# A two-layer diffusion backbone on one core: inputs fetched at once, a selector made on the chip, idle matmuls during the loads, and a new order of issue

## The chip, the core and the metric

The kernel runs on one NeuronCore of a Trainium2 chip. The metric is the device time of one launch in microseconds (us). A profile is one execution recorded by the hardware profiler; its span runs from the core's first instruction to its last, and the launch's own time is a little longer than the span. The engines are called as the profile calls them: PE is TensorE's matmuls, PEld its weight loads, DVE is VectorE, ACT is ScalarE, POOL is GpSimd, and SP is the queue that issues every DMA here.

## What is computed

A latent of 512 tokens by 1024 features and a context of 256 tokens pass two layers. Layer 0 mixes tokens by windowed grouped attention (16 query heads, 4 key heads of 64, band of 384 keys plus all 256 context keys, a sink logit for each head); layer 1 mixes them by a chunked gMLP. A SwiGLU network with 2816 hidden features follows each. RMS norms stand before and after each part, and a modulation (shift, scale, gate) comes from a conditioning vector through a 1024 by 6144 matrix for each layer. Only the latent is returned, and the context's own result of layer 0 is not needed.

```python
for i in range(DEPTH):
    mod_l = silu(c) @ ada_w[i] + ada_b[i]          # sh, sc, g for the mixer and for the FFN
    mod_c = silu(c_ctx) @ ada_w[i] + ada_b[i]
    h_l = modulate(rmsnorm(x, norm_g[i, 0]), sh_ml, sc_ml)
    h_c = modulate(rmsnorm(ctx, norm_g[i, 0]), sh_mc, sc_mc)     # layer 0
    y_l = mixer(h_l, h_c)                           # attention in layer 0, gMLP in layer 1
    x = x + g_ml * rmsnorm(y_l, norm_g[i, 1])
    f_l = swiglu(modulate(rmsnorm(x, norm_g[i, 2]), sh_fl, sc_fl), ffn_w_in[i], ffn_w_out[i])
    x = x + g_fl * rmsnorm(f_l, norm_g[i, 3])
return x
```

## The kernel before

All tensors are float32. A large product is made of three matmuls on a reduced-precision type: each operand is split into a high part (a cast, on ACT) and a low part (the difference, on DVE or POOL), and `mm3` (L216 to L219) or `mm_a` (L221 to L225) adds high by high, high by low and low by high in PSUM. So each 128 by 1024 half of a weight unit needs a DMA into a `raw` buffer (two of them, shared with the modulation's matrices), `Stream.high` on ACT (L173) and `Stream.low` on DVE or POOL (L176).

**The first stage** ends with the keys, values and first queries. The six 128-token tiles (four of x, two of the context) come by `x_fetch` (L409) into buffers of the tag `stg`, of which there are four. Each is squared on ACT (`square_in`, L191), gets its reciprocal root on DVE and POOL (`rstd_in`, L198 and L201), is multiplied by it on DVE (`norm_in`, L422), turned by eight 128 by 128 transposes on PE (`turn_in`, L431) and copied out of PSUM (`turned_in`, L438 and L443). For each of eight groups k of 128 features, `ada0_fetch` brings a 1 MB piece of the modulation matrix, `ada0_rows` (L454) multiplies it by the conditioning vectors, four groups of PE columns at a time, `ada0_rows_out` (L459) copies the partial rows, `ada0_cols` (L465) adds them and turns them into columns by a product with the selector `sel`, and `ada0_done` (L471, L472) makes scale and shift. `modulate0` (L480) applies them to group k of the latent on DVE, `modulated_high` casts the result on ACT, `modulated_low` takes the rest on DVE; the `_ctx` steps (L492) do the same for the context with tiles `hfc` and `hc`. Then `kv` (L217 to L219) adds group k's share to the keys and values of six tiles, and `q_first` that of the first queries. `sel` is a 128 by 2 tile, zero but for four rows in each quarter, which come by four DMAs of 4 by 2 numbers.

**The attention stage** makes 16 blocks of scores (L813, L814), bounds (L820), exponentials (L825), normalised probabilities (`normalise`, L841 on POOL), transposes (L847, L854) and values (L867), with the queries of the next heads (`q_step`, into `q_ps`) between them. The weight units of the queries are 2 to 5; their low parts are made on POOL in quarters of 128 by 512. **The first down projection** (`down`, L1090) follows: `work` steps add the attention's output into `y`, a `Chain` for each of four token tiles adds it to x (L1052), normalises and shifts (L1064, L1068), turns the tile (L1075) and splits it into H (`turned_hi` on ACT, `turned_lo` on DVE), and `head` starts the SwiGLU on tile after tile (`fa`). In the chains of tiles 2 and 3 a `merge` (L1036) comes first.

**The order** of the first stage, the attention and the first down projection is written out by hand. Every step is put into `plan` with `at(time, step)` (L519), and `run_plan` (L527) issues the steps in the order of the table `ORDER` (L41 to L156). What the table says is the order on each engine's queue and on SP's; engines then run freely and wait for each other by semaphores. The rest of the program (the two SwiGLU networks and the gMLP) is in plain code order.

## Time and profile before

| | us |
|---|---|
| median of three runs | 1191.85 |
| lowest and highest run | 1189.71, 1191.92 |
| the profiled execution's own time | 1185.71 |
| its span | 1183.9 |
| PE busy | 1150.2 |
| DVE, ACT and POOL busy | 648.9, 448.6, 205.0 |

A row of the profile's timeline, or of its chain of waits, begins with the start in us from the span's start and the duration in us; then come engine, line, operation, and the tiles written and read. In a row of the chain `issue` is time in which the engine waited for nothing that the profile shows. A row of the windows view gives, for a stretch of time, the busy time of each engine with its count of instructions, the granted TensorE clock as a share of full speed, the mean busy share of the 16 DMA engines, and GB/s. Matmuls are pipelined: a 128 by 512 matmul lasts 0.39 us in the timeline, but at full clock the next starts 0.23 us after it.

### The profile page before, as it was taken

To read this page: it belongs to the slowest core of one execution; us is meant where nothing else is said; L and a number is where in the kernel's file an instruction comes from. 1 tells how busy PE (TensorE), PEld (TensorE's weight loads), DVE (VectorE), ACT (ScalarE), POOL (GpSimd) and SP (SyncE) were. 2 spreads that over 40 slices of the span, in tenths; PEclk is the share of its full clock that TensorE was granted. 3 is DMA by queue.
4 is the path that set the end of the run, shared out by engine and by line. 5 is a ranking of instruction groups with operands and counts; after the bars stand their busy time and mean duration, and the time that the engine had idled before them with its cause. 6 is when DMAs were issued, how large, how long until landed. Compare 5 with 4: busy or idle time off the path is not lost.

```text
span 1183.9 us, 14683 instructions
## 1 busy us (share of the span) xinstructions
PE 1150.2 (97%) x5904; PEld 955.5 (81%) x5904; DVE 648.9 (55%) x902; ACT 448.6 (38%) x726; POOL 205.0 (17%) x187
## 2 busy tenths in 40 slices
PE   5999999999999999999999899999999999999997
PEld 4789888678988888888888788888888888878886
DVE  4788988866454657633446656546463223323234
ACT  6347677654322322322323444245122222213222
POOL 1437456417000000000003413024000000000000
PEclk9999999999999999999999899999999999999999
DMA  8742331252254576634343243231362232232221
GB/s 325 266 164 90 113 107 67 72 182 86 77 212 175 183 279 227 235 108 142 109 145 138 90 165 112 80 107 36 110 224 98 102 107 102 77 106 76 103 71 71
DMA packets 24744, 157.98 MB, mean 133 GB/s; under 512 B 3290, under 2 KB 3546, under 8 KB 7396
## 3 DMA queue, kind: packets, MB, share of 16 engines
q1 hardware_dynamic: 24676, 157.04, 37.7%
q8 instruction: 46, 0.75, 0.2%
q14 instruction: 22, 0.18, 0.0%
HBM read 154.94 MB, written 2.10 MB: 133 GB/s over the span
## 4 chain that ended last, share of the span: by engine, by line
PE 66%; issue 18%; DVE 8%; DMA 3%; ACT 2%; POOL 2%; DVEq 0%; POOLq 0%; SPq 0%; ACTq 0%
PE y L225 12%; PE f L1249 10%; PE f L1248 10%; PE f L1250 10%; PE v L225 3%; PE o_ps L867 2%; PE pT_ps L847 2%; PE s_ps L813 2%; PE fa L219 1%; PE s_ps L814 1%; DVE x L1052 1%; DMA ada_raw<-in_ada 1%; PE fa L217 1%; PE fa L218 1%; PE q_ps L217 1%
## 5 line engine op out<-in xcount | busy, mean ns | idle before, releaser
L176 DVE TENSOR_TENSOR w_lo<-w_raw,w_hi 128x1024 fp32r<-128x1024 f32 x149 | 183.3, 1237 | 321.2 <-ACT w_hi L173 318.7
L173 ACT CAST w_hi<-w_raw 128x1024 fp32r<-128x1024 f32 x162 | 168.8, 1052 | 460.3 <-PE f L1249 258.6
L225 PE MATMUL y<-w_hi,st 128*128 128x512 f32 x928 | 250.6, 390 | 2.8 <-DVE act L1235 2.8
L1248 PE MATMUL f<-H,w_hi 128*128 128x512 f32 x640 | 249.5, 390 | 0.0
L1250 PE MATMUL f<-H,w_lo 128*128 128x512 f32 x640 | 249.2, 389 | 0.0
L1249 PE MATMUL f<-H,w_hi 128*128 128x512 f32 x640 | 249.0, 389 | 0.0
L225 PEld LDWEIGHTS y<-w_hi,st 128*128 128x128 f32 x928 | 173.8, 188 | 39.1 <-DVE act L1235 3.2
L225 PE MATMUL y<-w_lo,st 128*128 128x512 f32 x464 | 143.5, 389 | 0.0
L314 DVE SCALAR_TENSOR_TENSOR acc<-ada_raw,sc,acc 128x1024 f32<-128x1024 f32 x80 | 106.0, 1325 | 66.4 <-DMA ada_raw<-in_ada 61.0
L1249 PEld LDWEIGHTS f<-H,w_hi 128*128 128x128 f32 x640 | 120.2, 188 | 25.0
L1250 PEld LDWEIGHTS f<-H,w_lo 128*128 128x128 f32 x640 | 120.1, 188 | 25.0
L1248 PEld LDWEIGHTS f<-H,w_hi 128*128 128x128 f32 x640 | 120.1, 188 | 24.9
L201 POOL TENSOR_TENSOR ry<-ry,mhalf 128x1 f32<-128x1 f32 x16 | 12.3, 771 | 582.9 <-DVE ry L198 579.4
L225 PEld LDWEIGHTS y<-w_lo,st 128*128 128x128 f32 x464 | 87.1, 188 | 18.1
L841 POOL TENSOR_SCALAR p<-p,st 128x512 f32<-128x512 f32 (+1 forms) x64 | 52.8, 840 | 45.8 <-DVE st L837 27.8
L820 DVE CUSTOM_DVE_ANT_0 s_ps<-s_ps,mask,nsink 128x512 f32<-128x512 f32 (+1 forms) x64 | 52.0, 819 | 13.4 <-PE s_ps L814 8.6
L825 ACT ACTIVATE p<-s_ps,st 128x512 f32<-128x512 f32 (+1 forms) x64 | 47.5, 743 | 16.0 <-DVE st L820 13.4
L305 POOL MEMSET acc<- 128x1024 f32 x10 | 9.5, 953 | 201.3 <-DVE acc_st L176 199.8
L176 POOL TENSOR_TENSOR w_lo<-w_raw,w_hi 128x512 fp32r<-128x512 f32 (+1 forms) x23 | 37.1, 1619 | 31.4 <-ACT w_hi L173 31.4
L847 PE MATMUL pT_ps<-ident,p 128*128 128x128 f32 x288 | 41.4, 273 | 0.2 <-ACT pt L854 0.2
L813 PE MATMUL s_ps<-khi,qT 128*128 128x256 f32 (+1 forms) x128 | 40.5, 329 | 0.2
L219 PE MATMUL fa<-w_lent,H 128*128 128x256 f32 x128 | 36.5, 285 | 4.2 <-DVE H L176 4.1
(201 smaller groups left out, 1685.3 us busy)
## 6 DMA issues: line engine op xcount, KB each, us to landing
w_raw<-in_w SPq DMA_DIRECT2D x87, 1024.0 KB, 4.8
ada_raw<-in_ada SPq DMA_DIRECT2D x40, 1024.0 KB, 4.9
ada<-in_ada SPq DMA_DIRECT2D x8, 1024.0 KB, 7.4
row<-in_norm_g SPq DMA_DIRECT2D x7, 512.0 KB, 6.1
xin<-in_x SPq DMA_DIRECT2D x4, 512.0 KB
x<-in_x SPq DMA_DIRECT2D x4, 512.0 KB, 3.6
out<-x SPq DMA_DIRECT2D x3, 512.0 KB, 2.6
xin<-in_ctx SPq DMA_DIRECT2D x2, 512.0 KB, 4.8
```

The lines of the kernel that those rows point to most:

```text
L173: nc.scalar.copy(out=hi, in_=src)
L176: (eng or nc.vector).tensor_tensor(out=lo, in0=src, in1=hi.bitcast(F32), op=ALU.subtract)
L219: nc.tensor.matmul(dst, ll, rh, start=False, stop=last)
L225: nc.tensor.matmul(dst, l, w[:, n * 512:(n + 1) * 512], start=first and i == 0, stop=last and i == 2)
L314: nc.vector.scalar_tensor_tensor(out=ac, in0=w, scalar=sc[:, k:k + 1], in1=ac, op0=ALU.mult, op1=ALU.add)
L813: nc.tensor.matmul(dst, self.qT[:, j, :], khi[:, self.g, k0:k0 + (c1 - c0) * P], start=True, stop=False)
L820: nc.vector.tensor_tensor_reduce(out=s, in0=s, in1=self.msk, scale=-1.0, scalar=nsink[:, h:h + 1], op0=ALU.add, op1=ALU.min, accum_out=sel ...
L841: nc.gpsimd.tensor_scalar(out=p, in0=p, scalar1=self.st[:, 12 + j:13 + j], scalar2=1.0, op0=ALU.mult, op1=ALU.mult)
L847: nc.tensor.transpose(ps[:, j * P:(j + 1) * P], self.probs[j][:, i * P:(i + 1) * P], ident)
L1248: nc.tensor.matmul(dst, hi, H[:, k, :], start=k == 0, stop=False)
L1249: nc.tensor.matmul(dst, hi, H[:, KC + k, :], start=False, stop=False)
L1250: nc.tensor.matmul(dst, lo, H[:, k, :], start=False, stop=k == KC - 1)
```

## The change

The tiles of the context go into buffers of their own (tag `vec`), so that all six input tiles are fetched without waiting for a buffer. `sel` comes out of the identity matrix, by two additions on DVE in place of a memset and four DMAs. A zeroed tile `idle` feeds matmuls into PSUM tiles that are written over later: five `warm` steps of 128 by 512, and one of 128 by 256 before the first transposes of a context tile and before the first `ada0_rows`. `norm_in` works on half tiles. `turned_in` makes one copy of 128 by 512 in place of two of 128 by 256, and which engine makes it changes. `modulated_high` makes H's high part on ACT from the transposed x with scale and shift, no longer from DVE's `hf`, which stays for the low part. The keys' rotation writes in place and one addition writes both copies; the context's keys are copied twice on ACT instead of once on ACT and once on DVE; the keys are split in halves. The table `ORDER` is another for all that it covers.

The core of the diff (of the table, its first line):

```diff
-x_fetch_1 x_fetch_2 square_in_2 square_in_1 x_fetch_3 dma#2 square_in_3 dma ada0_fetch_0 rstd_in_2 <lambda>
...
     sel = base.tile([P, 2], F32, name="sel")
-    nc.vector.memset(sel, 0.0)
...
-    xnT = [vec(f"xnT{i}") for i in range(4)]
+    xnT = [big(f"xnT{i}") for i in range(2)]
...
     def x_fetch(t):
-        xin[t] = base.tile([P, D], F32, name="xin", tag="stg", bufs=4)
+        xin[t] = base.tile([P, D], F32, name="xin", tag="stg", bufs=4) if t < NT else vec("xin")
...
-    def norm_in(t):
-        nc.vector.tensor_scalar(out=xin[t], in0=xin[t], scalar1=r0[t], scalar2=None, op0=ALU.mult)
+    def norm_in(t, h):
+        v = xin[t][:, h * 512:(h + 1) * 512]
+        nc.vector.tensor_scalar(out=v, in0=v, scalar1=r0[t], scalar2=None, op0=ALU.mult)
...
+    idle = first_p.tile([P, SEQ], F32, name="idle")
+    nc.vector.memset(idle, 0.0)
+
+    def fill(ps):
+        nc.tensor.matmul(ps, idle[:, 0:P], idle[:, 0:ps.shape[-1]], start=True, stop=True)
+
+    def warm(i):
+
+        if i == 0:
+            turned["warm"] = bankA("warm")
+        fill(turned["warm"])
...
+        if t == 4 and h == 0:
+            fill(ps[:, 0:256])
...
+        copy = nc.scalar.copy if t == 1 or t > 2 and h == 0 else nc.vector.tensor_copy
         if t < NT:
-            for q in range(2):
-                (nc.vector.tensor_copy if t % 2 else nc.scalar.copy)(
-                    out=xnT[2 * h + q].rearrange("p (k s) -> p k s", k=2)[:, :, t * P:(t + 1) * P],
-                    in_=pv[:, 2 * q:2 * q + 2, :])
+            copy(out=xnT[h].rearrange("p (k s) -> p k s", k=4)[:, :, t * P:(t + 1) * P], in_=pv)
         else:
-            c = slice((t - NT) * P, (t - NT + 1) * P)
-            nc.scalar.copy(out=cnT[:, 4 * h:4 * h + 4, c], in_=pv)
+            copy(out=cnT[:, 4 * h:4 * h + 4, (t - NT) * P:(t - NT + 1) * P], in_=pv)
+
+    def select():
+
+        i4 = ident.rearrange("p (q s) -> p q s", q=4)[:, :, 0:4:2]
+        s2 = small(4, "sel2").rearrange("p (q z) -> p q z", q=2)
+        nc.vector.tensor_tensor(out=s2, in0=i4[:, 0:2, :], in1=i4[:, 2:4, :], op=ALU.add)
+        nc.vector.tensor_tensor(out=sel, in0=s2[:, 0, :], in1=s2[:, 1, :], op=ALU.add)
...
     def modulated_high(k):
-        high(HA[:, k, :], h_mod[k])
+        xk = xnT[k // 4][:, (k % 4) * 512:(k % 4 + 1) * 512]
+        nc.scalar.activation(out=HA[:, k, :], in_=xk, func=AF.Identity, scale=sb0[k][:, 2:3], bias=sb0[k][:, 0:1])
...
-    for q in range(4):
-        at(0, dma, sel[32 * q:32 * q + 4, :], a["sel"])
+    for i in range(5):
+        at(.01 * i, warm, i)
+    at(4, select)
...
-            src = kv_part(t, 0).rearrange("p t (h d) -> p t h d", h=KVH)
-            nc.scalar.copy(out=doubled(t, 0), in_=src)
-            nc.vector.tensor_copy(out=doubled(t, 1), in_=src)
+            for z in range(2):
+                nc.scalar.copy(out=k_rows[t][:, z * 512:(z + 1) * 512].rearrange("p (h w d) -> p h w d", h=KVH, w=2),
+                               in_=kv_part(t, 0)[:, z, :].rearrange("p (h d) -> p h d", h=KVH).unsqueeze(2).to_broadcast([P, KVH, 2, HD]))
...
     def k_add(t):
-        m = k_raw[t][:, 512:1024].rearrange("p (t h d) -> p t h d", t=2, h=KVH)
-        for w in (1, 0):
-            nc.vector.tensor_tensor(out=doubled(t, w), in0=doubled(t, 0), in1=m, op=ALU.add)
+        nc.vector.tensor_tensor(out=k_rows[t].rearrange("p (n w d) -> p n w d", w=2, d=HD), in0=twice(k_raw[t][:, 0:512]),
+                                in1=twice(k_raw[t][:, 512:1024]), op=ALU.add)
```

Three places of the new order. **The first loads.** SP's queue from the second row on: `xin` is a tile of x or of the context, `ada_...` a 1 MB piece for one group k, `w_raw` weights of the keys and values. Before:

```order
L170 DMA xin<-in_x 128x1024 x3
L170 DMA cols<-in_cols 128x24
L170 DMA ident<-in_ident 128x128
L170 DMA ada_119<-in_ada 128x2048
L170 DMA xin<-in_x 128x1024
L170 DMA sel<-in_sel 4x2 x4
L170 DMA bu<-in_bu 128x8
L170 DMA xin<-in_ctx 128x1024 x2
L170 DMA ada_169<-in_ada 128x2048
L170 DMA w_raw<-in_w 128x1024
```

And now:

```order
L171 DMA xin<-in_ctx 128x1024
L171 DMA xin<-in_x 128x1024
L171 DMA ident<-in_ident 128x128
L171 DMA xin<-in_ctx 128x1024
L171 DMA cols<-in_cols 128x24
L171 DMA xin<-in_x 128x1024 x3
L171 DMA ada_183<-in_ada 128x2048
L171 DMA w_raw<-in_w 128x1024
L171 DMA ada_211<-in_ada 128x2048
L171 DMA ada_244<-in_ada 128x2048
```

The context's tiles moved to the front, all six tiles now stand ahead of the first piece of the modulation matrix, and two more pieces follow the first half unit of weights. On PE the first `kv` matmuls stood, before, behind two products `rows`:

```order
L454 MATMUL rows<-ada_169,s_90 32x256 x8
L465 MATMUL cols<-sel,rows 128x2 x2
L431 MATMUL xT<-ident,xin 128x128 x12
L217 MATMUL kv<-w_hi,HA 128x512
L218 MATMUL kv<-w_lo,HA 128x512
```

Now they stand here, and the first six are of the context (`hc`):

```order
L475 MATMUL rows<-ada_183,s_89 32x256 x8
L446 MATMUL xT<-ident,xin 128x128 x4
L486 MATMUL cols<-sel,rows 128x2 x2
L446 MATMUL xT<-ident,xin 128x128 x16
L475 MATMUL rows<-ada_211,s_89 32x256 x8
L218 MATMUL kv<-w_hi,hc 128x512
```

The second `rows` product still comes before the first `kv`, but its `cols`, which before stood between them, now come after. **The query weights of unit 5** in the attention, on POOL: `w_lo` rows are quarters of that unit, `p` rows are normalised probabilities. Before:

```order
L176 TENSOR_TENSOR w_lo<-w_raw,w_hi 128x512
L841 TENSOR_SCALAR p<-p,st 128x512 x2
L176 TENSOR_TENSOR w_lo<-w_raw,w_hi 128x512
L841 TENSOR_SCALAR p<-p,st 128x512 x2
L652 TENSOR_TENSOR qr<-qsb,rope 128x8x32 x2
L841 TENSOR_SCALAR p<-p,st 128x640 x5
L176 TENSOR_TENSOR w_lo<-w_raw,w_hi 128x512
L841 TENSOR_SCALAR p<-p,st 128x640
L176 TENSOR_TENSOR w_lo<-w_raw,w_hi 128x512
L841 TENSOR_SCALAR p<-p,st 128x640 x2
```

And now:

```order
L868 TENSOR_SCALAR p<-p,st 128x512 x4
L868 TENSOR_SCALAR p<-p,st 128x640 x4
L177 TENSOR_TENSOR w_lo<-w_raw,w_hi 128x512
L868 TENSOR_SCALAR p<-p,st 128x640 x3
L177 TENSOR_TENSOR w_lo<-w_raw,w_hi 128x512
L868 TENSOR_SCALAR p<-p,st 128x640
L177 TENSOR_TENSOR w_lo<-w_raw,w_hi 128x512 x2
```

The last four `p` rows are block 6's and the four ahead of them block 5's. The first quarter now stands behind block 5's probabilities, the second behind three of block 6's four, the last two behind all four; before, two quarters stood among block 4's and the other two among block 6's. **The chains of the first down projection**, on DVE: `y_part` is the merge of tile 2 or 3, `x` the addition to x, `H` a half of a tile's low part. Before:

```order
L1068 SCALAR_TENSOR_TENSOR tmp<-tmp,rx,row 128x512
L1048 TENSOR_TENSOR tmp<-y_part,row 128x1024
L176 TENSOR_TENSOR H<-hT,H 128x4x128 x2
L1052 SCALAR_TENSOR_TENSOR x<-tmp,ry,x 128x1024
L176 TENSOR_TENSOR H<-hT,H 128x4x128
L1036 TENSOR_TENSOR y_part<-y_3078,y_part 128x1024
L176 TENSOR_TENSOR H<-hT,H 128x4x128
```

And now:

```order
L1095 SCALAR_TENSOR_TENSOR tmp<-tmp,rx,row 128x512 x2
L177 TENSOR_TENSOR H<-hT,H 128x4x128 x2
L1063 TENSOR_TENSOR y_part<-y_3057,y_part 128x1024
L1079 SCALAR_TENSOR_TENSOR x<-tmp,ry,x 128x1024
L1075 TENSOR_TENSOR tmp<-y_part,row 128x1024
L177 TENSOR_TENSOR H<-hT,H 128x4x128 x2
```

Both halves of tile 0 now stand ahead of tile 2's addition to x (before, one of the two stood behind it), and three operations of the full width stand ahead of tile 1's halves.

More of the change, by code (lines that the diff above doesn't have):

```diff
@@ L156 @@
+c2gain_x c2rstd_x c3square_y c3rstd_y head_1_0 c2shift_x_0 c2shift_x_1 c3add_x c2turn_0 head_0_2 c2turn_1
+c2turned_hi_0 c3gain_x c3square_x c3rstd_x c2turned_hi_1 head_1_1 c2turned_lo_0 c2turned_lo_1 whigh_12_1 head_2_0
+c3shift_x_0 c3shift_x_1 head_1_2 c3turn_0 c3turn_1 c3turned_hi_1 c3turned_hi_0 c3turned_lo_0 wlow_12_0 c3turned_lo_1
+head_2_1 wlow_12_1 head_3_0 head_2_2 head_3_1 head_3_2
 """.split()
@@ L450, in ada0_rows @@
         rows0[k] = ps = bankA("rows")
+        if k == 0:
+            fill(ps[:, 0:256])
         for h in range(2):
@@ L548, in backbone_kernel @@
         at(b + 1.1, rstd_in, t)
-        at(b + 1.75, norm_in, t)
+        for h in range(2):
+            at(b + 1.75 + .1 * h, norm_in, t, h)
         for h in range(2):
@@ L579, in backbone_kernel @@
         at(W + 1.4 + i, rstd_in, t)
-        at(W + 2.1 + i, norm_in, t)
+        for h in range(2):
+            at(W + 2.1 + i + .1 * h, norm_in, t, h)
         for h in range(2):
@@ L716, in k_rope @@
             nc.gpsimd.tensor_tensor(out=m[:, :, :, z, :], in0=src[:, :, :, 1 - z, :], in1=table(32 + 32 * z), op=ALU.mult)
-            nc.vector.tensor_tensor(out=k2[:, :, :, z, :], in0=src[:, :, :, z, :], in1=table(0), op=ALU.mult)
+        for z in range(2):
+            nc.vector.tensor_tensor(out=src[:, :, :, z, :], in0=src[:, :, :, z, :], in1=table(0), op=ALU.mult)
     def k_add(t):
-        m = k_raw[t][:, 512:1024].rearrange("p (t h d) -> p t h d", t=2, h=KVH)
-        for w in (1, 0):
-            nc.vector.tensor_tensor(out=doubled(t, w), in0=doubled(t, 0), in1=m, op=ALU.add)
+        nc.vector.tensor_tensor(out=k_rows[t].rearrange("p (n w d) -> p n w d", w=2, d=HD), in0=twice(k_raw[t][:, 0:512]),
+                                in1=twice(k_raw[t][:, 512:1024]), op=ALU.add)
     def v_copy(t):
@@ L735, in k_turn, with k_split @@
                                     k_rows[t][:, (z * KVH + h) * P:(z * KVH + h + 1) * P], ident)
-    def k_split(t):
-        split(khi[:, :, t * P:(t + 2) * P], klo[:, :, t * P:(t + 2) * P],
-              k_ps[t].rearrange("p (h s) -> p h s", h=KVH))
+    def k_split(t, g):
+        c = slice(t * P, (t + 2) * P)
+        split(khi[:, 2 * g:2 * g + 2, c], klo[:, 2 * g:2 * g + 2, c],
+              k_ps[t].rearrange("p (h s) -> p h s", h=KVH)[:, 2 * g:2 * g + 2, :])
     qTs, q_of, copies = {}, {}, {}
@@ L763, in backbone_kernel @@
         at(end + turn, k_turn, t)
-        at(end + turn + .9, k_split, t)
+        for g in range(2):
+            at(end + turn + .9 + 3 * g, k_split, t, g)
     b = end - 3.5
```

232 lines of the change are left out of this document (114 added, 118 removed).

## Prediction

> **What bounds the kernel now.** I read the page's first part, then the windows, then the chain of waits, which says what the windows' idle engine waits for. The page first: span, and PE's busy time.
>
> ```profile
> span 1183.9 us, 14683 instructions
> PE 1150.2 (97%) x5904; PEld 955.5 (81%) x5904; DVE 648.9 (55%) x902; ACT 448.6 (38%) x726; POOL 205.0 (17%) x187
> ```
>
> PE is idle for 1183.9 − 1150.2 = 33.7 us only. The windows (length, then PE, PEld, DVE, ACT, POOL busy, granted clock, DMA share, GB/s) say where the change meets this: three stretches at the start, one of the attention.
>
> ```profile
> 0.00:10.00 10.00, 0.51 (x3) 0.51 (x4) 1.92 (x11) 6.53 (x10) 1.77 (x6) 1.00 0.78 290
> 10.00:20.00 10.00, 6.50 (x51) 5.19 (x49) 5.90 (x16) 5.98 (x15) 2.92 (x5) 1.00 0.79 277
> 20.00:30.00 10.00, 9.34 (x66) 6.88 (x67) 6.71 (x14) 6.94 (x12) 0.49 (x2) 0.83 1.02 415
> 120.00:280.00 160.00, 158.44 (x1007) 123.67 (x1006) 129.16 (x260) 106.15 (x224) 76.75 (x84) 1.00 0.30 106
> ```
>
> The first 20 us hold 9.49 + 3.50 = 13.0 of the 33.7. In the attention PE is busy for 158.44 of 160 us: there a new order can win at most 1.6 us, but it can lose. The chain of waits over the start shows what holds the first `kv` (start, duration, what):
>
> ```profile
> 1.65 4.57 DMA xin<-in_x
> ...
> 9.49 3.30 PE xT L431 x16
> ...
> 12.81 4.76 DMA xin<-in_ctx
> ...
> 20.19 1.09 PE rows L454 x16
> ...
> 22.34 2.49 PE xT L431 x12
> 24.83 0.43 PE kv L217
> ...
> 26.07 0.23 PE kv L217
> ```
>
> An x tile lands at 6.22, 16 transposes free the buffers that the context's tiles need, the last of those DMAs starts at 12.81 and lands at 17.57, and everything behind it follows: squares, `rows`, and the context's twelve transposes. The timeline has the first `kv` at 24.48:
>
> ```profile
> 24.48 0.78 PE L217 MATMUL kv<-w_hi,HA 128*128 128x512 f32 x1
> ```
>
> From there PE runs almost without a pause until the query steps (the start of the queries, below), so what the first `kv` gains, the end gains, unless a load or DVE falls behind.
>
> **The loads and the first `kv`.** SP's queue before:
>
> ```profile
> 4.70 3.14 SPq L170 DMA_DIRECT2D sel<-in_sel  x4
> ...
> 11.50 1.65 SPq L170 DMA_DIRECT2D xin<-in_ctx  x2
> ```
>
> Four issues and the wait for a buffer go. In the new order SP waits for nothing in its first eleven transfers, and one transfer must still land before the first `kv`: the second piece of the modulation matrix, for the second `rows`. The first `x` tile behind a context tile is again the second big transfer, so I let it land at 6.22. Behind it come ident 64, a context tile 512, cols 12, three x tiles 1536, the first piece 1024, a half unit of weights 512, the second piece 1024: 4684 KB or 4.80 MB. At the 415 GB/s of 20 to 30 us that is 11.6 us: the second piece lands at 17.8, its product (1.09 above) ends at 18.9.
>
> The other way to the first `kv` goes through the first piece, of which all but 1.57 MB (half unit and second piece, 3.8 us) is down at 17.8 − 3.8 = 14.0. What follows it is in the timeline before:
>
> ```profile
> 21.98 1.05 ACT L173 CAST w_hi<-w_raw 128x1024 fp32r<-128x1024 f32 x1 [0.30 <-DMA w_raw<-in_w]
> 22.51 0.27 DVE L472 TENSOR_SCALAR sb<-cols,sc 128x2 f32<-128x2 f32 x1
> ...
> 23.06 1.23 DVE L176 TENSOR_TENSOR w_lo<-w_raw,w_hi 128x1024 fp32r<-128x1024 f32 x1 [0.28 <-ACT w_hi L173]
> ...
> 26.03 0.41 DVE L492 TENSOR_SCALAR hfc<-cnT,sb 128x256 f32<-128x256 f32 x1
> ...
> 27.02 0.42 DVE L176 TENSOR_TENSOR hc<-hfc,hc 128x256 fp32r<-128x256 f32 x1
> ```
>
> From the start of `rows` (20.19) to the end of `sb` (22.78) are 2.6 us, so 14.0 becomes 16.6. Then on DVE `hfc` 0.41, one copy of 128 by 512 out of PSUM 0.68 (row below), `w_lo` 1.23 and the low part `hc` 0.42: 19.3. `w_hi` is done sooner: its half unit lands 2.5 us before the second piece, at 15.3, and takes 1.05. So the first `kv` starts at 18.9 and runs freely from 19.3; I take 19.1. That is 24.48 − 19.1 = 5.4 us earlier. DVE then has to make H's low part of the latent; before, the context's tiles came only when PE had other work. I take off 0.2 for a short wait there: **−5.2 us**.
>
> Behind the first `kv`, pieces of the modulation are issued early too, and each group k keeps PE for 18 matmuls of 0.23 us (last chain row) and a `rows` of 1.09, 5.2 us, while its loads of 1.57 MB take 3.8: PE stays the bound.
>
> A rule speaks against the sum. The Trainium skill's page "DMA: Bandwidth & Descriptors", section Specifications, gives a limit of about 358 GB/s from HBM for each core. My estimate by that figure: 4.80 MB would take 13.4 us, the first `kv` would come at about 20.9, and the gain would be 3.4 us. The 415 GB/s of the row above disagrees, and the measurement decides.
>
> **Edits at nothing.** The idle matmuls run while PE waits (0.51 us busy in its first 10), and end before the first transposes. `sel` from the identity costs two additions of four columns on an idle DVE. H's high part from x leaves DVE the same work, ACT the same one instruction for each k. Keys' rotation and copies move between ACT and DVE under a PE that is busy throughout; if that cover is gone, a keys' copy more is one row of the kind of 0.68, of which two keys' tiles make at most 1.4 us.
>
> **The clock at the first `kv`.** The granted clock before:
>
> ```profile
> 22.00:24.00 2.00, 2.00 (x14) 1.64 (x14) 1.61 (x4) 1.62 (x3) 0.00 (x0) 0.62 0.97 403
> 24.00:26.00 2.00, 2.00 (x8) 1.71 (x8) 1.31 (x3) 1.68 (x3) 0.00 (x0) 0.53 1.06 444
> ```
>
> The first six `kv` cost 0.43 in place of 0.23 at 0.53 of the clock: 6 × 0.20 = 1.2 us. In the new order PE still waits for pieces of the matrix between 9 and 19 us, with products too short to fill it; I let the same 1.2 us stay. That idle matmuls take it away is a rival.
>
> **The start of the queries.** The waits of PE between 84 and 93 us, and the clock behind them:
>
> ```profile
> PE q_ps L218 <- POOL w_lo L176: 1.1, 1, 1.1
> PE q_ps L217 <- ACT w_hi L173: 0.8, 1, 0.8
> ```
>
> ```profile
> 86.00:88.00 2.00, 1.31 (x8) 1.31 (x9) 1.65 (x3) 1.99 (x4) 2.00 (x2) 0.83 0.00 0
> 88.00:90.00 2.00, 2.00 (x11) 1.96 (x11) 1.32 (x3) 1.34 (x4) 1.80 (x3) 0.50 0.00 0
> 90.00:92.00 2.00, 2.00 (x15) 2.00 (x15) 1.79 (x5) 2.00 (x6) 1.84 (x2) 0.81 0.00 0
> ```
>
> The waits are 1.9 us; the clock costs 1.31 × 0.17 + 2 × 0.50 + 2 × 0.19 = 1.6. On ACT the query's copies stand ahead of `w_hi`, on POOL the rotation ahead of `w_lo`, in both orders, so I leave these 3.5 us where they are.
>
> **Unit 5.** Its quarters now stand behind probabilities. The groups of 120 to 240 us (busy, mean ns), and steps of PE in the chain of waits:
>
> ```profile
> L841 POOL TENSOR_SCALAR p<-p,st 128x640 f32<-128x640 f32 x24 | 22.7, 960 | 17.1 <-DVE st L837 13.2 <-ACT pt L854 2.3 <-PE s_ps L814 1.7
> ...
> L854 DVE COPY pt<-pT_ps 128x512 f32<-128x512 f32 x26 | 17.7, 682 | 0.7 <-PE pT_ps L847 0.5
> ...
> L176 POOL TENSOR_TENSOR w_lo<-w_raw,w_hi 128x512 fp32r<-128x512 f32 x10 | 13.1, 1311 | 10.0 <-ACT w_hi L173 10.0
> ```
>
> ```profile
> 145.46 0.44 PE pT_ps L847 x4
> 145.90 0.12 PE s_ps L813
> ...
> 154.58 1.87 PE o_ps L867 x8
> ```
>
> From block 6's reciprocals POOL needs 3 × 0.96 + 1.31 + 0.96 + 2 × 1.31 = 7.8 us until the last quarter. PE's steps from there to the `q_step` that needs it are, by the new order, six of queries (three matmuls of 0.12), three of scores (four of 0.12), three turns of 0.44 and the 1.87: 2.2 + 1.4 + 1.3 + 1.9 = 6.8. PE waits 7.8 − 6.8: **+1.0 us**. POOL may be ahead (0) or two instructions more behind (3.0), with a drop of the clock as at 86 us on top.
>
> **The down projection.** Timeline rows of tile 0 and 1 of the chains, and PE's wait:
>
> ```profile
> 267.09 1.29 DVE L1052 SCALAR_TENSOR_TENSOR x<-tmp,ry,x 128x1024 f32<-128x1024 f32 x1
> ...
> 275.70 1.22 DVE L1036 TENSOR_TENSOR y_part<-y,y_part 128x1024 f32<-128x1024 f32 x1
> ...
> 279.66 5.37 POOL L176 TENSOR_TENSOR w_lent<-w_raw,w_lent 128x1024 fp32r<-128x1024 f32 x2
> ...
> 282.84 3.28 DVE L1052 SCALAR_TENSOR_TENSOR x<-tmp,ry,x 128x1024 f32<-128x1024 f32 x1
> ...
> 286.05 0.68 DVE L176 TENSOR_TENSOR H<-hT,H 128x512 fp32r<-128x512 f32 x1
> ...
> 286.78 0.38 PE L219 MATMUL fa<-w_lent,H 128*128 128x256 f32 x1 [1.87 <-DVE H L176]
> ```
>
> Tile 2's addition to x takes 3.28 in place of 1.29 beside POOL's 5.37, and tile 0's second half stands behind it; PE waits 1.87. Now both halves stand ahead of it: −1.9. But tile 1's halves now stand behind a merge (1.22), the addition (1.29 to 3.28), a product as wide as the merge (1.22 again) and are two of 0.68: 5.1 to 7.1 us. PE has tile 0's 48 matmuls of 0.12, 5.8 us: a wait of 0 to 1.3, I take 0.7. Net **−1.2 us** (−1.9 to +1).
>
> **The sum:** −5.2 + 1.0 − 1.2 = −5.4. On the profiled execution 1185.71 − 5.4 = 1180.3. The median of the three runs, 1191.85, lies 6.1 above that execution; I let the same difference hold, 1191.85 − 5.4 = **1186.4 us**. 0.2% is 2.4 us, about what a measurement of this kernel can tell from no change.
>
> **The rivals.**
>
> *The loads come slower* (0.13). The first 10 us show 290 GB/s, the second ten 277, the latter with a pause of SP. If six tiles and two pieces together come at 290, 4.80 MB take 16.6 us, the second `rows` ends at 23.9, and the front gives 0.6 in place of 5.2: 1191.85 − 0.6 + 1.0 − 1.2 = 1191.0, no change that can be told. Against it: 403 to 444 GB/s in the rows from 22 us on.
>
> *The idle matmuls hold the clock* (0.06): the 1.2 us of the first `kv` go too, 1185.2. The rows above speak against it: at 22 us the clock was down although PE had been busy for 6.50 of the ten microseconds to 20. The Trainium skill's page "TensorE: Matmul & The Clock Gate", section "Part 1: The HAM clock gate", says that the array falls back to half speed after an idle window of about 3.4 us; the idle matmuls before 9 us would then be forgotten at 19, and the clock row at 22 agrees with a fall.
>
> *The pause before the queries goes* (0.16): the new order gives ACT or POOL the lead there, and 3.5 us more are won: 1182.9.
>
> *The attention's low parts fall behind* (0.08), the side of slower. What unit 5 meets may befall other units whose quarters moved behind probabilities: PE then stops, and the clock drops, each 3.5 us as at 84 to 92. At three places: −5.4 + 10.5 = +5.1, 1197.0. It decides from the third place; two end within 0.2%. For it: PE has only 1.6 us of slack in 160. Against it: POOL is busy for 76.75 of 160 us.
>
> **How the numbers follow.** My forecast has 0.57, its own range 1184.5 to 1188.5 by unit 5 (0 to +3) and the chains (−1.9 to +1). The range reaches down to the idle matmuls and the pause won together (1181.7) and up to the slow loads (1191.0): 1181.5 to 1191.2. Faster by over 0.2%: 0.57 + 0.06 + 0.16 = 0.79; within: 0.13; slower: 0.08.
>
> **What would show it.** Right: the context's DMAs start before 5 us, the first `kv` at 18 to 20, PE's waits for `w_hi` and `w_lo` of some 1.9 us still there at about 79, a wait of about 1 us for `w_lo` between 148 and 153, and no 1.9 us wait of `fa` for H. Wrong: a first `kv` at 22 or later with the DMA share below 0.9 before it; a `kv` stage in which PE waits for DVE's `HA` or a piece; PE waits for POOL's `w_lo` beyond unit 5, with clock rows of 0.5 behind them.

## The result, and the profile after

The changed kernel takes 1176.24 us (median of four runs, 1175.88 to 1176.54), the kernel before 1190.78 (four runs, 1187.90 to 1191.92). The ratio is 0.9881, with a 95% interval of 0.9862 to 0.9901: 14.5 us less, where 5.4 were forecast, and below the range of 1181.5 to 1191.2. The profiled execution of the changed kernel took 1176.41, its span is 1174.6. One further run of the kernel before, in the second group below, took 6589.16 us and is left out of every ratio.

Two gaps are to be explained. From profile to profile the span fell by 9.3 us and not by 5.4. And the profiled execution of before, 1185.71, was faster than any of its timed runs here, while that of the changed kernel lies among its own.

The page of the changed kernel, its first lines:

```profile
span 1174.6 us, 14699 instructions
...
PE 1153.4 (98%) x5918; PEld 955.5 (81%) x5918; DVE 647.9 (55%) x909; ACT 450.3 (38%) x723; POOL 210.0 (18%) x187
```

PE is idle for 21.2 us in place of 33.7, and some 7.6 us of its busy time are idle matmuls (1.78 to 7.81, 9.50 to 10.52 and 14.14 to 14.74). So the matmuls that both kernels share, 5904 records in each profile, take 1153.4 − 7.6 = 1145.8 us in place of 1150.2: of the 9.3 us some 4.9 are waits less, and some 4.4 are the same work done faster. The windows (length, then PE, PEld, DVE, ACT and POOL busy, granted clock, DMA share, GB/s) that answer to those of before:

```profile
0.00:10.00 10.00, 7.68 (x20) 3.71 (x20) 2.62 (x13) 6.71 (x11) 1.62 (x7) 1.00 0.75 265
10.00:20.00 10.00, 8.29 (x77) 5.45 (x75) 8.48 (x22) 6.82 (x13) 3.19 (x5) 1.00 1.02 423
20.00:30.00 10.00, 9.84 (x82) 7.49 (x83) 9.01 (x20) 5.50 (x10) 2.40 (x1) 1.00 1.01 414
...
120.00:280.00 160.00, 158.84 (x1002) 124.64 (x1003) 130.23 (x258) 109.33 (x225) 85.52 (x84) 1.00 0.30 103
```

The loads run at 423 GB/s from 10 to 20 us, where before they paused (277). The clock is 1.00 from 20 to 30 us, where before it was 0.83, and the first `kv` stands at 19.95:

```profile
19.95 0.50 PE L218 MATMUL kv<-w_hi,hc 128*128 128x512 f32 x1
```

The starts of PE's stages in the two timelines show where the 9.3 us arise:

| PE's first matmul of | before | changed | difference |
|---|---|---|---|
| `kv` | 24.48 | 19.95 | −4.5 |
| scores | 83.23 | 79.99 | −3.2 |
| `y` of the first down projection | 248.04 | 242.80 | −5.2 |
| `fa` of the first SwiGLU | 283.08 | 277.16 | −5.9 |
| `f` of the first SwiGLU | 310.54 | 303.58 | −7.0 |
| end of the last `f` | 1054.95 | 1048.13 | −6.8 |
| end of the last `y` | 1177.71 | 1168.16 | −9.5 |

Between the first `kv` and the scores 1.3 us of the gain are lost again; no run isolates why. Between 310 and 1055 us nothing is gained or lost. The last step stood in no sum: 2.7 us in the last `y`, whose code and order the change leaves alone. The end of the last `f` and the start of the last `y`, in the timeline of before:

```profile
1054.56 0.39 PE L1250 MATMUL f<-H,w_lo 128*128 128x512 f32 x1
1057.71 0.72 PE L225 MATMUL y<-w_hi,st 128*128 128x512 f32 x2 [2.77 <-DVE act L1235]
```

And in that of the changed kernel:

```profile
1047.74 0.39 PE L1277 MATMUL f<-H,w_lo 128*128 128x512 f32 x1
1047.97 0.62 PE L226 MATMUL y<-w_hi,st 128*128 128x512 f32 x2
```

A wait of 2.77 us for `act` is gone. `act` is what DVE makes of an `f`, here of the last one; the first matmuls of `y` read an older tile, so no data makes them wait. What can is the place in PSUM: the last `y` tiles come from a pool that takes over the banks of the `f` tiles, and `y0` gets the first pair. In the built program of before the last `f` lies in banks 0 and 1, just there; in the changed one it lies in 4 and 5. The reason stands 800 us earlier: the four slots of the `f` tiles' pool are given to tiles in the order in which the program asks for them, and in the new table `work_2_3`, which asks for the slot of `y3`, comes ahead of `c0turn_0`, which asks for that of the first `hT`; before, it came behind. The two tiles swap slots, and tiles that follow them are placed differently. Where only the first down projection goes back to the old order (below), the last `f` lies in banks 0 and 1 again; there `y0` is kept off it by one more tile, and PE has no wait for `act`.

### The profile page after: what moved, and what is told of

Read it like the earlier page. It is cut to its first block, busy times and chain, and to the rows that moved or that the text cites. A ratio compares the mean times of both kernels' runs of the same rounds, so it can differ in the third digit from the quotient of the medians.

```text
span 1174.6 us, 14699 instructions
## 1 busy us (share of the span) xinstructions
PE 1153.4 (98%) x5918; PEld 955.5 (81%) x5918; DVE 647.9 (55%) x909; ACT 450.3 (38%) x723; POOL 210.0 (18%) x187
## 4 chain that ended last, share of the span: by engine, by line
PE 64%; issue 18%; DVE 8%; DMA 5%; ACT 2%; POOL 2%; SPq 0%; POOLq 0%; DVEq 0%; ACTq 0%
PE y L226 13%; PE f L1275 10%; PE f L1276 10%; PE f L1277 10%; PE v L226 3%; DMA ada<-in_ada 3%; PE o_ps L894 2%; PE pT_ps L874 2%; DMA ada_raw<-in_ada 1%; PE s_ps L840 1%; PE s_ps L841 1%; PE fa L220 1%; DVE w_lo L177 1%; PE fa L218 1%; PE fa L219 1%
## 5 line engine op out<-in xcount | busy, mean ns | idle before, releaser
L868 POOL TENSOR_SCALAR p<-p,st 128x512 f32<-128x512 f32 (+1 forms) x64 | 55.9, 887 | 43.6 <-DVE st L864 21.6
```

What stands on the lines that cost most here:

```text
L868: nc.gpsimd.tensor_scalar(out=p, in0=p, scalar1=self.st[:, 12 + j:13 + j], scalar2=1.0, op0=ALU.mult, op1=ALU.mult)
```

## The experiments

Fifteen kernels ran in four groups, each group on one chip together with the kernel before, whose medians there were 1189.6, 1190.3, 1188.8 and 1189.2. "Free bank" below means that `y0` of the last product is kept off the last `f` by one more tile in its pool.

| kernel | us (median) | ratio to before, 95% |
|---|---|---|
| before again | 1189.70 | 0.9995 [0.9983, 1.0007] |
| before, `y0` in a free bank | 1185.33 | 0.9962 [0.9948, 0.9977] |
| before, context fetched at once | 1187.33 | 0.9985 [0.9975, 0.9996] |
| changed code, old order, free bank | 1187.59 | 0.9986 [0.9975, 0.9998] |
| the same, selector early | 1186.06 | 0.9982 [0.9972, 0.9993] |
| changed, old order up to the scores | 1186.83 | 0.9973 [0.9961, 0.9984] |
| changed, old order from the scores on, free bank | 1179.29 | 0.9913 [0.9896, 0.9929] |
| changed, old order of the first down projection, free bank | 1178.35 | 0.9905 [0.9889, 0.9921] |
| changed, `y0` on the last `f` | 1179.94 | 0.9914 [0.9898, 0.9930] |
| changed, no idle matmuls | 1178.89 | 0.9906 [0.9890, 0.9921] |
| changed, H's high part from `hf` | 1179.11 | 0.9928 [0.9913, 0.9942] |
| the same, one low part on DVE | 1176.70 | 0.9892 [0.9871, 0.9913] |
| changed again | 1176.83 | 0.9899 [0.9882, 0.9916] |
| changed, `y1` moved, idle matmuls before `v` | 1174.30 | 0.9883 [0.9870, 0.9896] |
| the same, two low parts on DVE | 1170.56 | 0.9840 [0.9823, 0.9858] |

The kernel before scatters over 6 us. The four first runs of the changed one lie within 0.7 us, but of six more, on another chip, two took 1178.93 and 1180.06; its medians were 1176.24 and 1176.83. Kernels near the changed one are compared by their medians, and a difference under 1 us between two of them is not clear of this scatter.

**The kernel before once more**, with no edit.

> The kernel before, unchanged, once more, for a second profile. Theory (clock): its time varies by some 4 us because the granted clock falls in the pauses before the first kv and before the queries, and comes back sooner or later; the second profile then shows 0.5 rows of another length at 22 to 30 and 84 to 95 us, and away from these places the steps lie within 0.5 us of the first profile's. Rival (loads): the context's DMA lands at another time, the first kv starts more than 1 us away from 24.5, and the clock rows are alike.

Its profiled execution took 1191.55 with a span of 1189.8, 5.9 more than the first. By PE's timelines 2.2 of these have arisen by the first scores, 2.7 by the first `y` and 3.0 by the end of the last `f`; the rest comes in the last `y`. Windows of this second profile, at the first `kv` and at the last `y`:

```profile
26.00:28.00 2.00, 2.00 (x6) 1.54 (x5) 1.92 (x5) 0.94 (x3) 0.00 (x0) 0.50 1.02 430
...
1060.00:1062.00 2.00, 1.33 (x3) 1.14 (x4) 0.62 (x2) 0.00 (x0) 0.00 (x0) 0.50 0.41 90
1062.00:1064.00 2.00, 2.00 (x6) 1.52 (x6) 0.00 (x0) 0.00 (x0) 0.00 (x0) 0.50 1.00 422
```

The last `y` in the first profile of before:

```profile
1060.00:1062.00 2.00, 2.00 (x11) 1.65 (x10) 0.00 (x0) 0.00 (x0) 0.00 (x0) 1.00 0.56 234
```

And its first matmuls in the second profile:

```profile
1060.67 1.22 PE L225 MATMUL y<-w_hi,st 128*128 128x512 f32 x2 [2.77 <-DVE act L1235]
```

The same wait of 2.77 us is followed by a clock of 0.50 in one execution (6 matmuls in 2 us) and of 1.00 in the other (11). At the first `kv` the clock is down for longer too (0.50 up to 28 us, where it was 1.00 from 26 on), and at the queries 0.64 and 0.51 stand from 90 to 94. The expectation's clock theory holds, with one addition: the last `y` is a third such place, which it had not named and which makes the largest part, and the first `kv` itself came 1.0 us later.

**Another bank for `y0`, in the kernel before and in the changed one.** A further tile takes the first slot of the last pool; on DVE it costs one memset of one column.

```diff
                 if k == 1 and pend:
                     self.gated(*pend.pop())
+                    if head is None:
+                        nc.vector.memset(self.pe.tile([P, D], F32, name="skip", tag="b2", bufs=3)[:, 0:1], 0.0)
...
-                pe = psE.__enter__()
+                pe = self.pe = psE.__enter__()
```

> The kernel before, with one more tile in the last pool of PSUM, so that y0 of the last down projection lies in banks 4 and 5 and not in 0 and 1, where the last f lies. Theory (banks): PE's wait of 2.8 us for act at the last y is gone, y0 starts right behind the last f, and the time falls by 2.5 to 2.9 us. Rival (act is needed there by the data, and something else made it earlier in the changed kernel): the wait stays between 2 and 3 us, the time stays.

> The changed kernel with the same extra tile: there the last f lies in banks 4 and 5, so y0 now lies on it. Theory (banks): PE waits 2.8 us for act ahead of the last y, the time rises by 2.3 us over the changed kernel (a wait of 0.5 for y1 goes), to about 1178.5. Rival: no change, 1176.2.

In the kernel before, `y` now starts right behind the last `f`:

```profile
1056.66 0.39 PE L1250 MATMUL f<-H,w_lo 128*128 128x512 f32 x1
1056.89 0.84 PE L225 MATMUL y<-w_hi,st 128*128 128x512 f32 x3
```

In the changed kernel, where the same edit puts `y0` on the last `f`, the wait appears, and half the clock behind it (four matmuls in 1.91 us where the row above has three in 0.84):

```profile
1051.32 0.74 PE L226 MATMUL y<-w_hi,st 128*128 128x512 f32 x2 [2.54 <-DVE act L1262]
...
1052.44 1.91 PE L226 MATMUL y<-w_hi,st 128*128 128x512 f32 x4
```

The times move by −4.2 (1189.6 to 1185.3) and +3.7 (1176.2 to 1179.9): the bank is the cause, and the price is the wait and the clock that it often pulls down. Both expectations had only the wait, and both were too small. The scatter of before shrinks with it, from 1186.8 to 1192.8 down to 1184.9 to 1185.9 in its five runs, so the last `y` seems to have made most of it.

**The changed kernel without its idle matmuls.** All calls of `warm` and `fill` are removed, and the idle tile; one unused bank keeps the rotation.

```diff
-        fill(turned["warm"])
...
-            fill(ps[:, 0:256])
```

> The changed kernel without its seven idle matmuls. Theory (clock): without them PE is idle until 7 us and in pauses behind, the granted clock is near 0.5 at the first kv (20 us) and the first six kv take 0.43 each: the time rises by 1 to 3 us, and its runs spread wider than the changed kernel's 0.7 us. Rival (the transposes keep the clock themselves): clock 1.00 from 20 us on as with them, time within 0.5 us of 1176.2.

Time 1178.89, +2.7. The clock at the first `kv` is 1.00 all the same, so the theory's mechanism fails there. What the idle matmuls change comes before: twelve transposes and the first `rows`, without them and with them.

```profile
12.62 2.82 PE L434 MATMUL xT<-ident,xin 128*128 128x128 f32 x12 [0.62 <-ACT cnT L443]
...
15.38 1.65 PE L461 MATMUL rows<-ada,s 128*32 128x256 f32 x16
```

```profile
12.77 1.53 PE L446 MATMUL xT<-ident,xin 128*128 128x128 f32 x12 [1.08 <-ACT cnT L455]
...
14.82 1.07 PE L475 MATMUL rows<-ada,s 128*32 128x256 f32 x16
```

Without them the first transposes run at about half speed, and `rows` is slower too. The windows show a granted clock of 1.00 there, as they do for the first 20 us of before, where the first 16 transposes take 3.29 us (16 at 16.85 in the changed kernel take 2.17). So that column does not show this slowness; that it is the clock all the same is inferred from the spacing of like instructions. The first `kv` comes at 21.09, 1.1 us later. The rest is a wait of 1.8 us for DVE that ends at 31.51, where a step of 0.40 us took 2.48 beside POOL; the experiment on H's high part explains it.

**Which part of the order.** Three kernels with the changed code and parts of the old table: all of it; only from the first scores on; only up to the first scores. Names that are split now stand as both halves in the old place, and `warm` at the front. Where the old order of the first down projection is in, the tile of the edit above frees the bank.

```diff
-x_fetch_4 square_in_4 x_fetch_1 square_in_1 warm_0 rstd_in_4 warm_1 dma rstd_in_1 x_fetch_5
+warm_0 warm_1 warm_2 warm_3 warm_4 x_fetch_1 x_fetch_2 square_in_2 square_in_1 x_fetch_3 dma#2
```

> The changed code with the order of before (half steps put where the whole one stood, the selector ahead of its first use, the five idle matmuls at the front), and y0 of the last product in a free bank, so it stands against the kernel before with the extra tile (1185.3). Theory (the order carries the front): the context's tiles still stand behind the first piece of the modulation on the queue and only lose the wait for a buffer, so the first kv comes 1 to 3 us earlier than 24.5 to 25.5; 1182 to 1184.5. Rival (the edits carry it): first kv at 20 or earlier, 1180 or less.

> The changed code with the new order up to the first scores and the order of before from there, y0 in a free bank. Theory (front and bank are nearly all of it, attention nothing, the chains 1 to 2 us): first kv at 20.0 as in the changed kernel, time 1177 to 1178.5. Rival (the new order of the attention is worth 2 us or more by itself): 1179 or above.

> The changed code with the order of before up to the first scores and the new order from there. Theory: the whole is the sum of its parts, so it loses against the changed kernel what the first of these kernels loses at the front, 2 to 4 us: 1178.5 to 1180.5. Rival (a late front is given back later, in pauses of the attention): within 1 us of 1176.2.

With the whole old order the edits gain nothing: 1187.6 against 1185.3 for before with a free bank, and the first `kv` at 25.2, where 1182 to 1184.5 were expected. With the new order up to the scores the first `kv` is at 19.94 and the time 1179.3. With the old front and the new rest it is 1186.8, nearly all of the loss. By the order of the front the two pairs differ by 1187.6 − 1179.3 = 8.3 and 1186.8 − 1176.2 = 10.6 us, far over the 2 to 4 that the theory had for the last, and the first kernel fell short of its 1 to 3 us at the first `kv`. Part of that is an accident of both kernels with the old front: PE waited for the selector, which had been put right ahead of its use. The row of the first:

```profile
PE cols L485 <- DVE sel L461: 2.6, 1, 2.6
```

**The selector early**, its two additions ahead of `rstd_in_2`:

> The kernel with the changed code in the order of before, y0 in a free bank, with the selector's two additions put ahead of the first rstd of tile 2 and no longer right ahead of their use. There PE waited 2.6 us for the selector. Theory: that wait goes, the first kv comes about 1 us earlier, and the time falls from 1187.6 by 0.5 to 1.5 us, so the edits in the old order still do not beat 1185.3. Rival (the selector alone made that kernel slow): 1185 or less.

1186.06, by 1.5 less, the first `kv` at 23.08: as the theory had it. All edits in the old order thus stand 0.7 above before with a free bank, which is no gain that can be told, and the order of the front is worth 1186.1 − 1179.3 = 6.8 us.

**The fetch alone, in the kernel before.** Only SP's queue and the buffer change:

```diff
-        xin[t] = base.tile([P, D], F32, name="xin", tag="stg", bufs=4)
+        xin[t] = base.tile([P, D], F32, name="xin", tag="stg", bufs=4) if t < NT else big("xin")[:, 0:D]
...
-x_fetch_1 x_fetch_2 square_in_2 square_in_1 x_fetch_3
+x_fetch_1 x_fetch_2 x_fetch_4 x_fetch_5 square_in_2 square_in_1 x_fetch_3
```

> The kernel before with one thing changed: the context's two tiles have buffers of their own (in the tag big) and stand third and fourth on SP's queue, so no transfer waits for a buffer; the order of all other steps is that of before. Prediction's step (the buffer wait and the loads hold the first kv): by the loads the second piece is down at about 17 and the weights' low part at about 20, so the first kv comes at 20 to 21.5 in place of 24.5 to 25.5 and the time falls by 3 to 5 us. Theory now (the order of the steps on PE and DVE holds it as well, since the context's squares, scalings and transposes stand behind those of all latent tiles): first kv at 22.5 to 25, time 0 to 2 us less.

Time 1187.33, ratio 0.9985: 1.5 us. The first `kv` starts at 23.94 in its timeline. Its chain of waits up to there:

```profile
18.14 1.55 PE xT L429 x12
...
20.58 1.41 DVE xin L420 x2
21.99 0.44 DVE HA L174
...
22.96 1.22 PE xT L429 x8
24.19 0.23 PE kv L215
```

The loads are down, but the context's scaling (`xin`, 20.58) and its transposes (22.96) stand where the old order put them, behind those of the latent and the second `cols`. The wait for a buffer was real and held little: the order behind it held the rest. In this profile the granted clock is 1.00 from 20 to 30 us, although nothing but the fetch was changed.

**The old order in the first down projection alone**, with a free bank.

```diff
-c2merge c1gain_x c1square_x c0turn_0 whigh_11_1 c1rstd_x
+c0turn_0 c1gain_x wfetch_12 c0shift_x_1 c1square_x c1rstd_x c2merge
```

> The changed kernel with the order of before in the first down projection alone, y0 in a free bank. Theory (the step of the prediction on the chains): PE waits about 1.9 us for H's low part of tile 0 again, as before the change, and the time rises by 1.2 to 1.7 us: 1177.4 to 1178. Rival (the 3.28 us addition came from something else than its place): no wait over 1 us, time 1176.2.

Time 1178.35, +2.1. Its DVE rows, and PE's wait:

```profile
276.92 3.29 DVE L1078 SCALAR_TENSOR_TENSOR x<-tmp,ry,x 128x1024 f32<-128x1024 f32 x1
280.13 0.68 DVE L176 TENSOR_TENSOR H<-hT,H 128x512 fp32r<-128x512 f32 x1
```

```profile
PE fa L219 <- DVE H L176: 1.9, 1, 1.9
```

The same addition in the changed kernel, with both of tile 0's halves ahead of it and tile 1's behind:

```profile
276.32 1.28 DVE L177 TENSOR_TENSOR H<-hT,H 128x512 fp32r<-128x512 f32 x2
...
278.65 1.27 DVE L1079 SCALAR_TENSOR_TENSOR x<-tmp,ry,x 128x1024 f32<-128x1024 f32 x1
...
280.98 1.28 DVE L177 TENSOR_TENSOR H<-hT,H 128x512 fp32r<-128x512 f32 x2
```

The step of the prediction holds, wait for wait. Its counterweight (0.7 us behind tile 1's halves) did not come, since the addition took 1.27. In the old order the clock fell behind the wait as well (0.74 from 280 to 285 us in its windows), which makes the price 2.1, somewhat over the 1.2 to 1.7 expected. With it the kernel at 1179.3 is read: it had reached the rival's figure, but by the chains' 2.1, which leaves 1179.3 − 1178.4 = 0.9 for the attention's order. That is within the scatter of four runs each, but the two profiles agree: the first `y` starts at 242.95 and 242.10.

**H's high part from `hf` again.** Four of the eight steps on ACT have to move behind DVE's; those moves in the table are not shown.

```diff
-        xk = xnT[k // 4][:, (k % 4) * 512:(k % 4 + 1) * 512]
-        nc.scalar.activation(out=HA[:, k, :], in_=xk, func=AF.Identity, scale=sb0[k][:, 2:3], bias=sb0[k][:, 0:1])
+        high(HA[:, k, :], h_mod[k])
```

> The changed kernel with H's high part made from hf again, as before the change (for four groups k the step on ACT then has to stand behind the one on DVE). Theory (nothing rests on it since PE is busy in the kv stage): within 0.7 us of 1176.2. Rival (DVE is what PE waits for there, and the high part from x took a link out of the chain): 1 to 3 us slower, with waits of PE for HA in the first 50 us.

Time 1179.11, +2.9: the rival. DVE waits 0.99 us for ACT there, which it does not in the changed kernel, and comes to the step below 1.05 us later. The rows of DVE, POOL and PE from its timeline:

```profile
27.69 2.57 DVE L512 TENSOR_SCALAR hfc<-cnT,sb 128x256 f32<-128x256 f32 x1
```

```profile
27.74 2.37 POOL L176 TENSOR_TENSOR w_lo<-w_raw,w_hi 128x1024 fp32r<-128x1024 f32 x1 [12.28 <-ACT w_hi L173]
```

```profile
31.51 0.50 PE L217 MATMUL kv<-w_hi,HA 128*128 128x512 f32 x1 [2.42 <-DVE xnT L452]
```

In the changed kernel the same step ends before POOL's begins:

```profile
26.64 0.40 DVE L514 TENSOR_SCALAR hfc<-cnT,sb 128x256 f32<-128x256 f32 x1
```

```profile
27.16 2.40 POOL L177 TENSOR_TENSOR w_lo<-w_raw,w_hi 128x1024 fp32r<-128x1024 f32 x1 [11.68 <-ACT w_hi L174]
```

A step of 0.40 us takes 2.57 where it meets POOL's 2.4, and all that is queued on DVE behind it is late by as much, the copy for which PE waits among it.

**The same with that low part on DVE**, and beside it the changed kernel once more.

```diff
-            at(n - .8, ws.low, KV0 + u, h, nc.gpsimd)
+            at(n - .8, ws.low, KV0 + u, h, nc.vector if u + 1 - h == 0 else nc.gpsimd)
```

> The changed kernel with H's high part from hf, as in the run before that cost 2.9 us, and with one half unit's low part (the one that POOL made at 27.7 us for 2.4 us) made on DVE instead. Theory (DVE stands still while POOL's long instruction runs): the hfc beside it takes 0.41 again in place of 2.57, PE's wait of 2.4 us for xnT goes or falls under 1 us although DVE now has 1.23 us of work more, and the time comes back by 1 to 3 us to 1176 to 1178. Rival (DVE is simply full there): the wait stays at 2 us or grows, 1179 or more.

> The changed kernel, unchanged, once more, on the chip of the next two. Theory (its gain does not hang on a lucky clock): 1175.5 to 1177, the first kv at 20 and no granted clock under 0.9 from 10 to 100 us, as in its first profile. Rival (the clock after the pauses at 78 to 86 us falls in some executions here too): a row of 0.5 to 0.7 near 85 us and 2 to 3 us more.

```profile
27.66 0.41 DVE L512 TENSOR_SCALAR hfc<-cnT,sb 128x256 f32<-128x256 f32 x1
```

```profile
PE kv L217 <- DVE xnT L452: 0.2, 1, 0.2
```

DVE has 1.22 us more to do there, and PE's wait falls from 2.4 to 0.2, the time from 1179.1 to 1176.7. POOL's long instruction made the wait, not a full DVE. The Trainium skill's page "SBUF — State Buffer", section "Who interferes with whom", says that DVE and GpSimd share a pair of ports, which some DVE instructions need, and that one instruction then holds the pair to its end while the other stands still. These rows agree, 0.41 against 2.57 us; their starts, 27.69 and 27.74, do not tell which of the two came first. Copies out of PSUM (0.68 at 27.57 in the changed kernel, with POOL busy) show none of it. The changed kernel once more took 1176.83 (1176.24 to 1180.06), with the clock at 1.00 up to 645 us in its profile: its gain does not hang on a lucky profile. Later its clock, too, falls in one execution and not in another: it is 0.50 from 804 to 806 us in this profile, where the first has 1.00.

**A faster version, in two steps.** First, `y1` leaves the bank of the last `f` (by the tile of the edit above, asked for ahead of `y1`; not shown), and twelve idle matmuls stand ahead of the first `v` of the gMLP, where PE waits for H:

```diff
             v_ps[t] = slot(f"v{t}")
+            if t == 0:
+                for _ in range(12):
+                    nc.tensor.matmul(v_ps[t][:, 0:P], ident, ident, start=True, stop=True)
```

> The changed kernel with y1 of the last product moved off the bank of the last f, and twelve idle matmuls of 128 by 128 ahead of the first v of the gMLP, where PE waits 1.5 us for H, then 1.8. Theory (clock): the wait of 0.5 at the last y goes, the granted clock from 650 to 660 rises from 0.58 and 0.74 to 0.9 or more, and the time falls to 1173.5 to 1175. Rival (the second wait of 1.8 us alone pulls the clock down): clock as it was, 1175.7.

Then two low parts, in the first SwiGLU's down projection alone, go from POOL to DVE:

```diff
-                at(b + 1, ws.low, u, h, nc.gpsimd if i in (2, 3) else nc.vector)
+                at(b + 1, ws.low, u, h, nc.gpsimd if i in (2, 3) and part else nc.vector)
```

> The version with y1 off the last f's bank and idle matmuls ahead of v, and with the two low parts of lent weights made on DVE in place of POOL in the down projection of the first SwiGLU alone. There an addition to x of 1.28 us took 3.42 beside POOL's 2.54, and PE waited 1.5 and 1.8 us for H. Theory (the same standstill): each of the two costs DVE 1.23 us and gives back about 2.1, PE's waits for H at the first v shrink by 1 us or more, and the time falls from 1174.3 by 0.5 to 2 us. Rival (DVE is the tighter engine there): the waits grow, 1174.5 to 1177.

The window behind that wait, in the changed kernel, then with the first step:

```profile
652.00:654.00 2.00, 2.00 (x6) 1.52 (x6) 1.35 (x2) 1.15 (x2) 1.10 (x1) 0.50 0.75 246
```

```profile
652.00:654.00 2.00, 2.00 (x15) 1.75 (x14) 0.78 (x3) 1.85 (x3) 1.83 (x1) 1.00 0.45 162
```

15 matmuls in place of 6 in the same 2 us: the clock stays up there, 1174.30. What each of the two edits of this step is worth was not told apart. With the second step the addition of 3.42 us beside POOL is 1.28 again. Changed kernel, DVE and POOL, then the second step:

```profile
641.39 3.42 DVE L1079 SCALAR_TENSOR_TENSOR x<-tmp,ry,x 128x1024 f32<-128x1024 f32 x1
```

```profile
641.19 2.54 POOL L177 TENSOR_TENSOR w_lent<-w_raw,w_lent 128x1024 fp32r<-128x1024 f32 x1
```

```profile
640.66 1.28 DVE L1079 SCALAR_TENSOR_TENSOR x<-tmp,ry,x 128x1024 f32<-128x1024 f32 x1
```

And from 600 us on its PE waits once, where the changed kernel waits three times (2.3, 1.8 and 1.5 us):

```profile
PE fa L220 <- DVE H L177: 1.4, 1, 1.4
```

1170.56 us (1170.29 to 1171.02), 6.3 below the changed kernel on the same chip and 0.9840 of before. The second step gives 3.7 us, more than the 0.5 to 2 that were expected: in windows of 5 us its granted clock never reads under 0.99 until PE's work ends, while the first step's profile has 0.50 from 800 to 802 us.

## Why the prediction was wrong, point by point

| term | forecast | measured, and by which kernels |
|---|---|---|
| front | −5.2 | −6.0: before with a free bank, 1185.3, to the new front in the changed code, 1179.3 |
| unit 5 (attention) | +1.0 | −0.9: 1179.3 to 1178.4 |
| chains of the first down projection | −1.2 | −2.1: 1178.4 to 1176.2 |
| the last `y` | none | −4.2: 1189.6 to 1185.3 |
| sum | −5.4 | −13.2 |

Unit 5 stands for the whole order of the attention in the measured column, and the front for the edits and the order together. The 1.3 us between this sum and the 14.5 of the result are about what the medians of before differ by from chip to chip (1188.8 to 1190.8).

**What bounds the kernel** held: PE, with its idle time at the start. But the list of PE's waits was read for the stages that the change touches. The 2.77 us for `act` at 1057 us stood in the profile of before, and the prediction put the last product at nothing, without a reason. The order table moves one allocation of a PSUM slot, and the last product inherits it: 4.2 us. This failing step is the largest term missed, and no rival named it.

**The median** was the second failing step: "I let the same difference hold", 6.1 us between the profiled execution and the median. That difference belongs to the clock of before, which falls at the first `kv`, at the queries and at the last `y` for longer or shorter; its execution in the profile was a lucky one. Where a change takes such waits away, the difference goes with them: the changed kernel's is 0.2, though single runs of it on the other chip lay up to 3.2 above their median. The forecast's own range was too narrow as well: 1184.5 to 1188.5 lets unit 5 or the chains reach their upper bound, and both together give 1190.7.

**The front** was right in size, and the first `kv` was forecast at 19.1 (measured 19.95; the first piece landed at 14.78, forecast 14.0). The reason was half right, and so the size was in part luck. The second piece, which was to be one of the two holders, made no wait: from the first `rows` at 14.82 PE goes without a pause through products and 20 transposes to the first `kv`, 5.1 us that the sum did not have. DVE's way, the other holder, was ready at about the same time (`w_lo` ends at 19.68, the low part of `hc` at 20.01). The chain showed the context's DMA waiting for a buffer, and the prediction made that the holder of all that follows; the fetch alone gave 1.5 us, the edits alone nothing, the order of squares, scalings and transposes behind it the rest.

**Edits at nothing** failed for two of them. "H's high part from x leaves DVE the same work" is true, and undoing it costs 2.9 us; "the idle matmuls run while PE waits" is true, and leaving them out costs 2.7. In both kernels DVE's step of 0.40 us comes too late, by 0.4 and 1.1 us, to be through before POOL's low part begins. The cover named, a PE that is busy throughout, was thin there; without H's high part from x the price was not that of the step but of the standstill beside POOL, and without the idle matmuls the standstill comes on top of the 1.1 us of slower transposes.

**The clock at the first `kv`** was forecast at half and is full. The rival on the idle matmuls got the outcome, for a wrong reason: without them it is full as well. What took the fall away is not shown. PE's stretch ahead of `kv` is fuller, busy for 8.29 us between 10 and 20 where before it was 6.50; but that alone does not decide, since 7.77 were followed by 0.50 in the second profile of before, and 7.82 by 1.00 in the kernel with the fetch alone.

**The start of the queries** kept as much waiting as forecast and lost the fall of the clock, so half of that rival came. Only one of the two waits is the one that was forecast to stay, for `w_lo` (1.0 us); that for `w_hi` is gone, and waits of the scores stand in its place. The changed kernel's waits between 68 and 100 us, and two windows behind them:

```profile
PE q_ps L219 <- POOL w_lo L177: 1.0, 1, 1.0
PE s_ps L840 <- ACT p L852: 0.9, 2, 0.7
PE s_ps L840 <- ACT qT L706: 0.7, 1, 0.7
```

```profile
86.00:88.00 2.00, 2.00 (x18) 2.00 (x17) 1.54 (x4) 0.88 (x5) 0.51 (x1) 1.00 0.33 49
88.00:90.00 2.00, 2.00 (x18) 1.97 (x17) 1.82 (x6) 1.76 (x5) 1.27 (x2) 1.00 0.89 344
```

2.6 us of waits in four pieces and a clock of 1.00; before, 1.9 us in two pieces and 0.50. The kernel without idle matmuls has 0.67 from 85 to 90 us. What decides between a fall and none is not settled here. The Trainium skill's page "TensorE: Matmul & The Clock Gate", section "Part 1: The HAM clock gate", has the gate watch a window that runs freely of the kernel; the two profiles of before, with the same 2.77 us wait and 1.00 or 0.50 behind it, agree with that.

**Unit 5** was mis-sized, +1.0 us where no such wait came: POOL's way to the last quarter and PE's to the step that needs it, in the changed kernel's timeline.

```profile
144.68 2.35 POOL L868 TENSOR_SCALAR p<-p,st 128x640 f32<-128x640 f32 x3 [3.19 <-DVE st L864]
...
149.03 2.52 POOL L177 TENSOR_TENSOR w_lo<-w_raw,w_hi 128x512 fp32r<-128x512 f32 x2
```

```profile
155.37 0.28 PE L219 MATMUL q_ps<-w_lo,HA 128*128 128x256 f32 x1
```

POOL takes 151.55 − 144.68 = 6.9 us and not 7.8, since the probabilities are 0.78 each there and not the mean of 0.96. PE comes for the second half of the unit only at 155.37, 10.7 us after POOL began and not 6.8: PE was further back in its order at that moment than the sum had it. That leaves 3.8 us of slack, and no wait.

**The chains** went the way that was forecast, by the wait that was forecast to go (1.9 us). The term is short, −1.2 where −2.1 were measured, because the wait behind tile 1's halves did not come and the fall of the clock behind the old wait was not counted.

## What to carry to other kernels

A wait of PE in code that a change leaves alone can hang on the change: look at every wait in the list. Where a first matmul waits for something that it does not read, look at which tile's PSUM bank it takes over. A profile is one execution; if the granted clock falls behind its pauses, the median lies elsewhere, and the price of a pause is the wait and the fall. Where a short DVE step reads several times its usual duration, look at POOL's row beside it before calling DVE full.
